# The first sublayer's start in another order: modulation in quarters, ten tiles on the operand without its norm, squares on GpSimd

## The chip, the cores and the metric

The kernel runs on one core of a Trainium2 chip. The metric is the device time of one execution in microseconds, as a median of runs. Six parts of the core matter: TensorE (PE, the matrix products), VectorE (DVE), ScalarE (ACT), GpSimd (POOL), SyncE (SP), which issues most of the loads, and the DMA engines that carry them.

## What is computed

One inference step of a network of two layers with shared weights for 128 context and 256 latent tokens of width 1024, kept on the chip as x with 384 columns. Each layer has three sublayers (feed-forward, mixer, feed-forward). What matters here is the first of all, with the modulation that scales and shifts its operand:

```python
def rmsnorm(x, g):
    r = lax.rsqrt(jnp.mean(xf * xf, axis=-1, keepdims=True) + EPS)
    return (xf * r).astype(x.dtype) * g

def swiglu(h, w13, w2):
    gate, up = jnp.split(h @ w13, 2, axis=-1)
    return (jax.nn.silu(gate) * up) @ w2

mod = jax.nn.silu(cond) @ w_mod[l] + b_mod[l]
sh1, sc1, gt1, ... = jnp.split(mod, N_MOD, axis=-1)
h = rmsnorm(x, g_norm[l, 0]) * (1.0 + sc1) + sh1
x = x + 0.5 * gt1 * swiglu(h, ffn1_w13[l], ffn1_w2[l])
```

`cond` differs between context and latent tokens, so each modulation vector has two columns. The feed-forward width is 2816.

## The kernel before, in words

Every product is made in float32 precision from halves: a number is split into a rounded high part and the low remainder. The high half of a weight is a copy on ACT (line 180), the low half a subtraction on DVE (line 183), 128x1024 each, and a product is three passes on PE (`mm3`, lines 232 to 234): high weight by high operand, low weight by high operand, high weight by low operand. **A step** is these three passes for one weight tile (128 of the 1024 rows of the output) and one of the eight parts (128 channels) of the operand. **A tile** is eight steps that add up in one PSUM buffer; its evacuation on ACT and DVE comes behind them. A feed-forward layer has 22 pairs of tiles (gate and up) in its first half. Weights come as one 512 KB load per tile through a ring of buffers; `split_upto` issues the high half at once and leaves the low half to be issued some steps later, or at once by `run_later(99)`. Jobs are generators that `step` runs one after the other, and each engine executes its instructions in the order in which the program writes them.

**The first group** (`start_group`, 287 to 370) has four tiles. `w_mod` of the scale and shift (8.4 MB) comes in four quarters; a quarter gives two of the eight parts. `products(q)` makes the sixteen small products of a quarter on PE (line 301, 256 columns, four rows of `scond` by tile position, so that four go side by side), ACT copies the result (309), `finish(q)` transposes it (316) and DVE sums it and makes `amod` (scale) and `modT` (shift). `make_h0` then scales and normalises the operand on DVE (555), adds the shift and rounds it on ACT (560), and takes the remainder on DVE (563). The norm itself is made first: squares of x on DVE and ACT at the program's start (`norm_sq`, 1190 to 1198), column sums on PE (526), the inverse root, and its broadcast to all partitions by PE (545, 546), copied as `rb` (548). So the four tiles work on the finished operand h. `warm(28)` and `warm(10)` are products without use (640) that keep PE busy.

The loads stand on SP's queue in the order x (four loads), first quarter (two loads of 1 MB), the four tiles' weights, quarters two, three and four; `cond` comes on ACT's queue.

**Later sublayers** of this kind start with `lead`: three tiles (`lead_group`) on the operand u, which is x scaled by `amod` without its norm, and 386 columns wide: the two last columns are the shift, so that their products give the shift's share apart. The norm is made meanwhile on PE (`norm_stats`, `norm_bcast`), and is applied to the result (`normed`, DVE, line 619) before the evacuation goes on with Silu on ACT (717). Five more tiles on u follow, and beside their steps `make_h` builds the normalised operand h with its scaling on POOL (575, 577) and its split on ACT and DVE (408, 411). From tile 9 on the tiles use h.

Behind the first tiles DVE makes the modulation of the other sublayers in the background (439), in pieces that `mods.put` hands out per tile: in the first sublayer over the tiles from number 8 on (counted from 0).

## Time and profile before

| | |
|---|---|
| median of 3 runs | 1919.38 us (1918.47 to 1919.88) |
| profiled execution | 1918.23 us, its span 1916.2 us |
| granted clock of PE, mean | 0.997 |
| busy share PE, its weight loads (PEld) | 99%, 97% |
| busy share DVE, ACT, POOL | 68%, 41%, 10% |

Times in the trace count from the start of the span. In the rows below, L301 is line 301 of the kernel before; "out<-in" are the program's names without buffer numbers, where S stands for buffers that share one pool (operands, and weights of the modulation's first quarters); "[0.24 <-DVE wlo L183]" says that the engine stood idle for 0.24 us just before and that the last thing it waited for was DVE's low half of a weight. Matmul records overlap one another: what a product costs in a row of equal ones is the distance of their starts, not the duration shown. The granted clock is a share of full speed: 1.00 is 2.4 GHz, 0.5 is 1.2 GHz.

### The profile page before, as it was taken

How to read it: one execution, taken by the hardware profiler on the slowest of the kernel's cores; microseconds unless marked ns; L12 is line 12 of the kernel's file. 1: busy time of each engine (PE TensorE's matmuls, PEld its weight loads, DVE VectorE, ACT ScalarE, POOL GpSimd, SP SyncE). 2: the span in 40 equal slices, each digit the busy share in tenths (PEclk: the TensorE clock that was granted, in tenths of full speed). 3: DMA queues.
4: the chain of work that ended last, by engine and by line, in shares of the span. 5: the costliest groups of instructions: out<-in, count | busy, mean ns of one | idle time of the engine just before them, and what ended most of it. 6: DMA issues, size and time to landing. Idle time of an engine off the chain costs nothing.

```text
span 1916.2 us, 28408 instructions
## 1 busy us (share of the span) xinstructions
PE 1903.4 (99%) x11024; PEld 1849.4 (97%) x11024; DVE 1308.7 (68%) x1948; ACT 789.7 (41%) x1412; POOL 198.5 (10%) x399
## 2 busy tenths in 40 slices
PE   8999999999999999999999999999999999999998
PEld 7999999889999999999999999998899999999998
DVE  5677885777656768778768779668766546655543
ACT  4433334445553444333334333354555534433332
POOL 0000003101221031000040000050022200400000
PEclk9999999999999999999999999999999999999999
DMA  8666663643335536566536656546433333354430
GB/s 331 197 200 194 219 207 128 214 131 112 98 100 173 162 112 201 189 197 223 181 109 221 192 192 223 170 137 200 123 111 103 102 123 130 111 172 157 154 110 34
DMA packets 91719, 308.69 MB, mean 161 GB/s; under 512 B 10816, under 2 KB 17600, under 8 KB 90816
## 3 DMA queue, kind: packets, MB, share of 16 engines
q1 hardware_dynamic: 90864, 306.17, 49.0%
q8 instruction: 87, 1.43, 0.3%
q10 hardware_dynamic: 720, 0.70, 0.1%
q14 instruction: 48, 0.39, 0.1%
HBM read 303.16 MB, written 3.67 MB: 160 GB/s over the span
## 4 chain that ended last, share of the span: by engine, by line
PE 98%; DMA 1%; DVE 0%; ACT 0%; issue 0%; DVEq 0%; ACTq 0%
PE mm L232 29%; PE mm L233 28%; PE mm L234 28%; PE mm L388 2%; PE mm L390 2%; PE mm L389 2%; PE sc L1009 2%; PE mm L1067 1%; PE tp L1050 1%; DMA S<-in_w_mod 1%; PE tp L835 1%; DMA gnorm<-in_g_norm 0%; PE ms L1096 0%; PE sc L301 0%; PE tp L640 0%; DMA cond<-in_cond 0%
## 5 line engine op out<-in xcount | busy, mean ns | idle before, releaser
L232 PE MATMUL mm<-S,whi 128*128 128x384 f32 (+1 forms) x3136 | 1063.8, 339 | 1.2 <-ACT S L560 1.2
L233 PE MATMUL mm<-S,wlo 128*128 128x384 f32 (+1 forms) x3136 | 1054.2, 336 | 0.2 <-DVE wlo L183 0.2
L234 PE MATMUL mm<-S,whi 128*128 128x384 f32 (+1 forms) x3136 | 1048.7, 334 | 0.0
L183 DVE TENSOR_TENSOR wlo<-raw,whi 128x1024 fp32r<-128x1024 f32 x424 | 520.6, 1229 | 239.9 <-ACT whi L180 239.2
L232 PEld LDWEIGHTS mm<-S,whi 128*128 128x128 f32 x3136 | 589.5, 188 | 14.0 <-issue 10.0
L234 PEld LDWEIGHTS mm<-S,whi 128*128 128x128 f32 x3136 | 588.8, 188 | 0.4 <-DVE S L563 0.4
L233 PEld LDWEIGHTS mm<-S,wlo 128*128 128x128 f32 x3136 | 587.6, 187 | 0.8 <-DVE wlo L183 0.6
L180 ACT ACTIVATE whi<-raw 128x1024 fp32r<-128x1024 f32 x424 | 445.5, 1052 | 199.6 <-PE mm L234 116.5
L439 DVE SCALAR_TENSOR_TENSOR acc<-raw,scond,acc 128x1024 f32<-128x1024 f32 x224 | 277.3, 1280 | 0.0
L408 ACT ACTIVATE S<-t 128x384 fp32r<-128x384 f32 x144 | 74.1, 523 | 329.7 <-DVE t L732 241.3
L509 POOL TENSOR_TENSOR yr<-yv,nhalf 128x3 f32<-128x3 f32 x9 | 9.6, 1062 | 1344.0 <-DVE yv L529 1016.6
L411 DVE TENSOR_TENSOR S<-t,S 128x384 fp32r<-128x384 f32 x144 | 83.8, 590 | 34.6 <-ACT S L408 34.6
L732 DVE TENSOR_TENSOR t<-t,mm 128x384 f32<-128x384 f32 x76 | 42.1, 554 | 77.8 <-PE mm L234 77.8
L713 ACT ACTIVATE t<-mm 128x384 f32<-128x384 f32 x76 | 37.3, 491 | 137.5 <-PE mm L234 137.5
L388 PE MATMUL mm<-whi,S 128*128 128x512 f32 x192 | 77.3, 403 | 0.0
L390 PE MATMUL mm<-whi,S 128*128 128x512 f32 x192 | 75.2, 392 | 0.0
L389 PE MATMUL mm<-wlo,S 128*128 128x512 f32 x192 | 75.1, 391 | 0.0
L577 POOL TENSOR_SCALAR t<-t,amod,modT 128x256 f32<-128x256 f32 x80 | 67.3, 850 | 4.2
L502 ACT ACTIVATE t<-x 128x384 f32<-128x384 f32 x44 | 22.9, 526 | 98.3 <-DVE x L627 98.3
L1100 DVE SCALAR_TENSOR_TENSOR S<-ms,sublng,S 128x128 fp32r<-128x128 f32 (+1 forms) x32 | 13.4, 418 | 65.3 <-ACT S L1099 65.3
L1026 ACT ACTIVATE e<-sc,ym 128x384 f32<-128x384 f32 (+1 forms) x96 | 47.7, 508 | 20.0 <-DVE ym L1016 20.0
L627 DVE SCALAR_TENSOR_TENSOR x<-mm,modT,x 128x256 f32<-128x256 f32 x96 | 35.6, 413 | 28.3 <-PE mm L234 28.0
(150 smaller groups left out, 1144.0 us busy)
## 6 DMA issues: line engine op xcount, KB each, us to landing
raw<-in_ffn_w SPq DMA_DIRECT2D x264, 512.0 KB, 4.2
raw<-in_w_mod SPq DMA_DIRECT2D x132, 512.0 KB, 4.6
raw<-in_w_in SPq DMA_DIRECT2D x112, 512.0 KB, 3.8
raw<-in_w_branch_a SPq DMA_DIRECT2D x16, 512.0 KB, 3.7
raw<-in_w_branch_b SPq DMA_DIRECT2D x16, 512.0 KB, 3.7
raw<-in_w_out SPq DMA_DIRECT2D x16, 512.0 KB, 3.7
S<-in_w_mod SPq DMA_DIRECT2D x6, 1024.0 KB, 10.7
x<-in_x SPq DMA_DIRECT2D x4, 384.0 KB, 4.2
```

Of the source, the lines that this page charges most:

```text
L180: S.activation(out=hi, in_=raw, func=AF.Copy)
L183: V.tensor_tensor(out=lo, in0=raw, in1=hi.bitcast(F32), op=ALU.subtract)
L232: T.matmul(ps, lhsT=w_hi, rhs=r_hi, start=first, stop=False)
L233: T.matmul(ps, lhsT=w_lo, rhs=r_hi, start=False, stop=False)
L234: T.matmul(ps, lhsT=w_hi, rhs=r_lo, start=False, stop=last)
L388: T.matmul(ps, lhsT=l_hi[:, kt, ts_], rhs=hi[:, sl], start=first, stop=False)
L389: T.matmul(ps, lhsT=l_hi[:, kt, ts_], rhs=lo[:, sl], start=False, stop=False)
L390: T.matmul(ps, lhsT=l_lo[:, kt, ts_], rhs=hi[:, sl], start=False, stop=last)
L408: S.activation(out=dst_hi, in_=src, func=AF.Copy)
L411: V.tensor_tensor(out=dst_lo, in0=src, in1=dst_hi.bitcast(F32), op=ALU.subtract)
L439: V.scalar_tensor_tensor(out=acc[n], in0=raw, scalar=s, in1=acc[n], op0=ALU.mult, op1=ALU.add)
L577: G.tensor_scalar(out=t[:, s0:s1], in0=t[:, s0:s1], scalar1=amod[:, i, kt, n:n + 1], scalar2=modT[:, l, pc_sh, kt, n:n + 1], op0=ALU.mult, ...
```

## The change

In the first sublayer the order of the work is now written out as a list of words, `START`, and that of the loads as another, `LOADS`:

- **Loads.** The first quarter comes ahead of x, and the quarters, parts of x and the four tiles' weights are interleaved. Each quarter comes in four loads of 512 KB. `b_mod` and `g_norm` stand with `cond` at the head of ACT's queue.
- **Products.** A quarter's sixteen products are made in four visits of four (`p00` to `p33`), one per load. All four quarters share one PSUM buffer. `finish` multiplies with a selection matrix (`tiled`) instead of transposing, and DVE makes scale and shift straight from PSUM.
- **Operand.** The four tiles work on u (`make_u`, 386 columns), and so do six more tiles behind them, with `make_h` beside: ten tiles on the operand without its norm, where there were none. `lead` does both groups; `make_h0` is gone. The exchange of two buffers' roles (`turn`) that later sublayers do now stands behind the first four tiles too.
- **Norm.** The squares are made on POOL (`q0` to `q7`, fifteen operations of 384 columns), the sums, the inverse root and the broadcast (`n0`, `n1`, `n2`) stand among the steps of the four tiles.
- **Warming products.** Ten ahead of the first visit, then groups of two to twelve (`w10`, `w3`, `w12` ...) between the visits.
- The background modulation of this sublayer starts at tile 10 instead of 8. The table of ACT's Silu function is loaded by a small dummy call at the start.

In `START` a word `s12` is a step of tile 1 with part 2, `p21` a visit of quarter 2 for its second load, `f1` finish of quarter 1, `u3` part 3 of the operand, `c2` the split of tile 2's weight (low half included), `e0` the evacuation of tile 0 and the split of the weight four tiles on. In `LOADS` `q1` is a quarter, `x2` two parts of x, and `c4` the weights' loads up to the fourth.

```diff
+LOADS = "q0 x0 c1 c2 x2 q1 c3 c4 x4 q2 x6 c7".split()
+START = (
+    "q0 q1 q2 q3 q4 q5 q6 q7 w10 p00 w3 p01 w3 p02 w3 p03 w2 f0 u0 c0 u1 c1 w12 s00 s01 s10 p10 s11 p11 w3 p12 "
+    "w3 p13 w2 f1 u2 u3 c2 c3 w5 s02 s12 s03 s13 s20 s21 p20 s22 s23 p21 s30 s31 p22 s32 p23 s33 f2 u4 u5 w2 "
+    "s04 s14 p30 s24 s34 p31 s05 p32 n0 s15 p33 s25 f3 u6 u7 n1 s35 s06 s16 s07 s17 n2 e0 e1 s26 s27 e2 s36 s37 e3"
+).split()
...
+            start_group(keys[:n0], evacs[:n0], l, i)
+            Job([], lambda c: iter_once(turn))
...
+        def products(at):
+            q, r = divmod(at, 10)
+            key = first_keys(q)[r]
+            for g in range(4):
+                T.matmul(
+                    st0["big"][32 * g:32 * g + 32, q % 2, 0:256], lhsT=scond[:, 4 * (r // 2) + g, 2 - 2 * (r % 2):34 - 2 * (r % 2)],
+                    rhs=raw_of[key][:, g * 256:(g + 1) * 256],
+                    start=r == 0, stop=r == 3, tile_position=(0, 32 * g))
...
         def finish(q):
+            m = tmp(256)
+            S.activation(out=m, in_=st0["big"][:, q % 2, 0:256], func=AF.Copy)
+            sel = st0["big"][:, q % 2, 256:264].rearrange("p (f c) -> p f c", f=2)
             for f in range(2):
+                T.matmul(sel[:, f, :], lhsT=m[:, f * P:(f + 1) * P], rhs=tiled[:, 0:4], start=True, stop=True)
+            for f in range(2):
+                k = 2 * q + f
+                V.scalar_tensor_tensor(
+                    out=amod[:, i, k, :], in0=sel[:, f, 0:2], scalar=gnorm[:, l, i, k:k + 1], in1=modT[:, l, SC1, k, :],
+                    op0=ALU.mult, op1=ALU.add)
...
+        def square(k):
+            if k == 0:
+                nst["acc"] = sp.tile([P, NT], F32, tag="at", name="acc")
+                G.tensor_tensor(out=nst["acc"], in0=x[:, k, :], in1=x[:, k, :], op=ALU.mult)
+            else:
+                sq = sp.tile([P, NT], F32, tag="qf", name="sq", bufs=2)
+                G.tensor_tensor(out=sq, in0=x[:, k, :], in1=x[:, k, :], op=ALU.mult)
+                G.tensor_tensor(out=nst["acc"], in0=nst["acc"], in1=sq, op=ALU.add)
...
+                elif what == "e":
+                    run_later(99)
+                    evacs[arg](pss[arg][:, :NU])
+                    split_upto(c + n + arg)
...
-        n_u = 0 if first else 8
-        n_0 = 4 if first else n_u
+        n_0 = 10 if first else 8
...
-        spread = 2 * NFF - 8
+        spread = 2 * NFF - n_0
...
-        for dt in range(4):
-            norm_sq(dt)
...
-            S.activation(out=sq, in_=x[:, dt, :], func=AF.Square)
```

**On PE, in the middle of the four tiles, before**: `mm_283` to `mm_286` are the four tiles' results, `sc_354` that of the second quarter's products, S0 and S1 the operand's halves, S6 and S7 buffers that hold the quarter.

```order
L232 MATMUL mm_286<-S0_150,whi_274 128x384
L233 MATMUL mm_286<-S0_150,wlo_275 128x384
L234 MATMUL mm_286<-S1_151,whi_274 128x384
L232 MATMUL mm_283<-S0_150,whi_203 128x384
L233 MATMUL mm_283<-S0_150,wlo_204 128x384
L234 MATMUL mm_283<-S1_151,whi_203 128x384
L301 MATMUL sc_354<-S6_112,scond_71 32x256 x4
L301 MATMUL sc_354<-S7_114,scond_71 32x256 x4
L301 MATMUL sc_354<-S6_112,scond_71 32x256 x4
L301 MATMUL sc_354<-S7_114,scond_71 32x256 x4
L232 MATMUL mm_284<-S0_150,whi_233 128x384
```

In before all sixteen products of a quarter stand in one row between two steps.

**The same place after**: `mm_143` and `mm_144` are the third and fourth tile, `sc_139` the result of the third quarter's products.

```order
L242 MATMUL mm_143<-S1_131,whi_308 128x386
L310 MATMUL sc_139<-S6_117,scond_71 32x256 x4
L240 MATMUL mm_144<-S0_130,whi_314 128x386
L241 MATMUL mm_144<-S0_130,wlo_315 128x386
L242 MATMUL mm_144<-S1_131,whi_314 128x386
L240 MATMUL mm_144<-S0_130,whi_314 128x386
L241 MATMUL mm_144<-S0_130,wlo_315 128x386
L242 MATMUL mm_144<-S1_131,whi_314 128x386
L310 MATMUL sc_139<-S7_120,scond_71 32x256 x4
L240 MATMUL mm_144<-S0_130,whi_314 128x386
L241 MATMUL mm_144<-S0_130,wlo_315 128x386
L242 MATMUL mm_144<-S1_131,whi_314 128x386
```

The sixteen are now four visits, with one or two steps of a tile between them.

**On ACT, around the last steps of the four tiles, before**: `t_493` is the Silu of the first tile (a gate, which becomes its product with the second tile), `whi_495` the high half of the fifth tile's weight, S0 the operand's high half, S2 the high half of that product.

```order
L560 ACTIVATE S0_150<-t_465,modT_78 128x256
L560 ACTIVATE S0_150<-t_465,modT_78 128x128
L713 ACTIVATE t_493<-mm_283 128x384
L180 ACTIVATE whi_495<-raw_262 128x1024
L408 ACTIVATE S2_504<-t_493 128x384
L713 ACTIVATE t_518<-mm_285 128x384
L408 ACTIVATE S2_504<-t_518 128x384
L180 ACTIVATE whi_529<-raw_278 128x1024
```

There the first tile's Silu and the split of the fifth tile's weight follow the operand's last part.

**The same place after**: `rb_494` is the broadcast norm, `t_496` the first tile's normalised result, `yb_497` its share of the shift, `whi_502` the high half of the fifth tile's weight, S2 again the high half of the product.

```order
L561 ACTIVATE rb_494<-ms_491 128x384
L716 ACTIVATE t_496<-t_496,yb_497 128x256
L716 ACTIVATE t_496<-t_496,yb_497 128x128
L188 ACTIVATE whi_502<-raw_237 128x1024
L421 ACTIVATE S2_508<-t_496 128x384
L188 ACTIVATE whi_517<-raw_312 128x1024
L716 ACTIVATE t_530<-t_530,yb_531 128x256
L716 ACTIVATE t_530<-t_530,yb_531 128x128
L188 ACTIVATE whi_536<-raw_318 128x1024
```

The fifth tile's weight now stands behind the norm's copy and the first tile's two Silu pieces.

**On POOL, at the program's start, before**: `ident` is the unit matrix, `yr` the norm's root of a later sublayer.

```order
masks.py:199 ISA
masks.py:199 AFFINE_SELECT ident_64<-ident_64 128x128
L509 TENSOR_TENSOR yr_193<-yv_191,nhalf_67 128x3
L509 TENSOR_TENSOR yr_2857<-yv_2855,nhalf_67 128x3
L575 TENSOR_TENSOR t_2969<-x_80,rb_2894 128x384
```

**After**: `acc` is the sum of squares, `sq` one square.

```order
masks.py:199 ISA
masks.py:199 AFFINE_SELECT ident_64<-ident_64 128x128
L337 TENSOR_TENSOR acc_145<-x_80 128x384
L340 TENSOR_TENSOR sq_147<-x_80 128x384
L341 TENSOR_TENSOR acc_145<-acc_145,sq_147 128x384
L340 TENSOR_TENSOR sq_150<-x_80 128x384
L341 TENSOR_TENSOR acc_145<-acc_145,sq_150 128x384
```

POOL now squares x in the first group, one square and one sum per part, where it had nothing to do before.

## Rows read from the trace of the kernel before

**Rows 1.** Waits of PE, whole span: times in total, count, longest, us.
```profile
PE sc L301 <- DMA S<-in_w_mod: 2.5, 2, 1.8
...
```

**Rows 2.** Stretches: length, busy us per engine, granted clock, DMA share, GB/s.
```profile
12.00:36.00 24.00, 20.75 (x166) 15.01 (x163) 14.14 (x40) 9.12 (x17) 0.80 (x1) 0.86 1.02 411
48.55:1916.20 1867.65, 1859.85 (x10695) 1813.64 (x10694) 1282.93 (x1875) 770.11 (x1373) 196.96 (x392) 1.00 0.49 157
```

**Rows 3.** PE in time order: start, duration, what, count, idle before and releaser.
```profile
12.92 2.79 PE L301 MATMUL sc<-S,scond 128*32 128x256 f32 x24 [0.71 <-DMA S<-in_w_mod]
...
20.34 0.42 PE L232 MATMUL mm<-S,whi 128*128 128x384 f32 x1
20.60 0.34 PE L233 MATMUL mm<-S,wlo 128*128 128x384 f32 x1
...
21.53 0.44 PE L233 MATMUL mm<-S,wlo 128*128 128x384 f32 x1 [0.24 <-DVE wlo L183]
...
37.17 0.33 PE L234 MATMUL mm<-S,whi 128*128 128x384 f32 x1
37.44 1.94 PE L301 MATMUL sc<-raw,scond 128*32 128x256 f32 x32
...
39.58 0.33 PE L233 MATMUL mm<-S,wlo 128*128 128x384 f32 x1
...
48.55 0.34 PE L232 MATMUL mm<-S,whi 128*128 128x384 f32 x1
...
49.07 0.34 PE L232 MATMUL mm<-S,whi 128*128 128x384 f32 x1
```

**Rows 4.** PE in time order, other stretches: warming products, norm sums, norm broadcast.
```profile
5.38 4.07 PE L640 MATMUL tp<-ones 128*128 128x128 f32 x35
...
310.98 0.73 PE L526 MATMUL ms<-ones,acc 128*128 128x2 f32 x6
...
316.12 0.60 PE L546 MATMUL ms<-t,ones 128*128 128x256 f32 x2
```

**Rows 5.** ACT and DVE by form: count | busy us, mean ns | idle.
```profile
L180 ACT ACTIVATE whi<-raw 128x1024 fp32r<-128x1024 f32 x424 | 445.5, 1052 | 199.6 <-PE mm L234 116.5 <-issue 55.7 <-PE mm L390 20.4
...
L548 ACT ACTIVATE rb<-ms 128x384 f32<-128x384 f32 x6 | 2.9, 492 | 30.0 <-PE ms L546 30.0
...
L309 ACT ACTIVATE t<-sc 128x256 f32<-128x256 f32 x4 | 1.5, 385 | 4.6 <-PE sc L301 4.6
...
L183 DVE TENSOR_TENSOR wlo<-raw,whi 128x1024 fp32r<-128x1024 f32 x424 | 520.6, 1229 | 239.9 <-ACT whi L180 239.2
...
L619 DVE TENSOR_TENSOR t<-mm,rb 128x384 f32<-128x384 f32 x24 | 13.1, 546 | 0.0
```

**Rows 6.** ACT in time order, the operand's high part for the first step.
```profile
19.05 0.80 ACT L560 ACTIVATE S<-t,modT 128x256 fp32r<-128x256 f32 x2 [0.28 <-DVE t L555]
```

**Rows 7.** PE by form, first of the three products.
```profile
L232 PE MATMUL mm<-S,whi 128*128 128x384 f32 x2816 | 954.0, 339 | 1.2 <-ACT S L560 1.2
...
L232 PE MATMUL mm<-S,whi 128*128 128x386 f32 x320 | 109.9, 343 | 0.0
```

**Rows 8.** POOL, then DVE, in time order, where POOL normalises an operand.
```profile
319.40 1.02 POOL L575 TENSOR_TENSOR t<-x,rb 128x384 f32<-128x384 f32 x1
...
321.49 1.98 POOL L575 TENSOR_TENSOR t<-x,rb 128x384 f32<-128x384 f32 x1
...
329.60 1.69 DVE L183 TENSOR_TENSOR wlo<-raw,whi 128x1024 fp32r<-128x1024 f32 x1 [1.82 <-ACT whi L180]
```

**Rows 9.** DVE in time order, a later layer's first eight tiles.
```profile
977.40 0.55 DVE L619 TENSOR_TENSOR t<-mm,rb 128x384 f32<-128x384 f32 x1
...
1002.12 1.23 DVE L183 TENSOR_TENSOR wlo<-raw,whi 128x1024 fp32r<-128x1024 f32 x1 [0.38 <-ACT whi L180]
...
1006.70 1.23 DVE L183 TENSOR_TENSOR wlo<-raw,whi 128x1024 fp32r<-128x1024 f32 x1 [1.88 <-ACT whi L180]
...
1010.79 2.55 DVE L183 TENSOR_TENSOR wlo<-raw,whi 128x1024 fp32r<-128x1024 f32 x2 [0.39 <-ACT whi L180]
```

199 lines of the change are left out of this document (71 added, 128 removed).

## The prediction

> **What bounds the kernel now.** I read three views in this order. First who keeps TensorE (PE) waiting: over the whole span there are four such groups, the dearest 2.5 us [rows 1]. Then the stretches: from 48.55 us to the end PE is busy 1859.85 of 1867.65 us [rows 2]. So the program is a start of 48.55 us and a rest that PE paces; whatever moves the instant at which the fifth weight tile begins moves the end by as much, and any new wait of PE behind it adds. Third the start itself on PE [rows 3]: the first step (three products of one weight tile with one of eight parts of the operand) begins at 20.34 (its second product at 20.60), the last of 32 steps ends at 48.55. One step in the steady state is 0.52 us (48.55 to 49.07) [rows 3], so 32 steps are 16.7 of these 28.2 us; the rest is modulation products, transposes and waits. The change rewrites this start and the six tiles behind it. Elsewhere only the pacing of the background modulation moves (26 pieces over 34 tiles instead of 36), which rests on VectorE (DVE) and is not waited for behind 48.55; I cost it at nothing.
>
> **When the first step can start.** In before the second load of the first quarter is what a product waits for until 12.92 [rows 3]; 3.67 MB were ordered up to it (1.57 of x, 2.10 of the quarter). Now the quarter comes first: 1.57 MB less, at 411 GB/s [rows 2] 3.8 us, so it is there at 9.1. Then, one behind the other: the last visit of products 0.5, the copy on ScalarE (ACT) 0.39 [rows 5], two selection products 0.5 (four records; six small ones take 0.73 [rows 4]), 0.3 allowed for three small DVE operations, on ACT the scaled operand in two pieces 0.80 [rows 6] and the weight's high half 1.05, on DVE its low half 1.23 [rows 5]. That is 14.2 for the second product of the first step. PE's own queue comes on top: ten warming products at the lower clock, then four visits with three warming products between them, which end about 1 us later than the load. I take 15.4, bounds 14.2 and 16.0; before it was 20.60 [rows 3], so **5.2 us earlier**.
>
> **What PE does from there to the end of the four tiles.**
> - Steps: 32 x 0.52, and 96 products of 386 instead of 384 columns, 4 ns longer each [rows 7]: 17.0 (before 16.7).
> - Visits to the modulation products. From 37.17 to 39.58 PE does two weight products and one visit of sixteen [rows 3]: 2.41, less two of 0.17, is 2.06 per visit. The sixteen are eight rounds; the last of the 32 records starts 1.94-0.38 = 1.56 after the first, so a round is 0.22 and eight are 1.73. Entering and leaving thus cost 0.33. Before: three visits inside this stretch, 6.2. Now four products per visit, twelve visits: 12 x (0.43+0.33) = 9.1. Lower bound 12 x 0.43 = 5.2 if the switch hides; I take 9.1, since the row shows the same neighbours.
> - Warming products on PE's queue: two groups of three in the second quarter stand between loads that have landed (1.8 us of loads apart, but PE is by then behind them). 4.07/35 = 0.116 per record [rows 4], two records each: 1.4. Those behind a quarter's last visit lie inside the next item.
> - From a quarter's last product to the next step: 0.39 + 0.5 + 0.3 + 0.8, with handovers 2.1. Behind quarter 1 nothing covers it (2.1), behind quarter 2 one step (1.6), behind quarter 3 two (1.1): 4.8. Before, the copies and transposes of later quarters stood beside steps; what PE waited there is part of its 28.2.
> - The norm: the sums 0.7 and the broadcast 0.6 [rows 4] now stand among the steps, before they stood ahead of 20.34: 1.3.
> - Waits for low halves on DVE, which makes the operand's eight low parts and four weights' while GpSimd (POOL) squares. Without POOL the rows show one such wait, 0.24 [rows 3]. Most of the twelve stand directly ahead of their step now: nine waits are 2.2, which I take; two are 0.5, twelve, with POOL's 0.46 (below) on two of them, 3.8.
> Sum 17.0+9.1+1.4+4.8+1.3+2.2 = 35.8. I count from the second product of the first step, so less 0.2: 15.4+35.6 = 51.0 against 48.55: **+2.5**. The 5.2 won by loading the quarter first are used up by more visits (2.9), warming (1.4), the norm (1.3) and gaps.
>
> POOL's squares themselves I cost at nothing on the path. Fifteen operations of this size take 1.02 each alone and up to 1.98 beside DVE [rows 8]. The last part of x is 9.96 MB down the queue: 12.92 + (9.96-3.67)/0.411 = 28.2, and four operations behind it give 32.3, 36.1 at 1.98 each. PE asks for the sum only behind the third of quarter 3's visits, near 40. Four microseconds cover it; without the cover the norm, and with it the evacuations, would be late by the difference.
>
> What POOL does to DVE is the other side: while POOL worked at 321.49 its operation took 1.98 instead of 1.02, and a weight's low half on DVE took 1.69 at 329.60 instead of 1.23 [rows 5, 8]. The Trainium skill (SBUF — State Buffer, Who interferes with whom) says why: a DVE instruction with two SBUF inputs and a GpSimd instruction that reads SBUF share one port pair, held for a whole instruction. The rows agree. By the rule, a low part that comes just behind a square's start stands for the whole 1.0 of it, and four such meetings would add 2 us to the 2.2 above; without the rule they would stay at 2.2 or under.
>
> **The turn from the fourth to the fifth tile.** Before, the first tile's evacuation and the fifth tile's split stand at once behind the first tile's end. Now both weight halves of the fifth tile sit on ACT and DVE behind the norm's broadcast: from the last product of tile 1 on, broadcast 0.6, its copy 0.49, the tile's scaling on DVE 0.55 and 0.1 allowed for a two-column copy, two Silu pieces 0.8 like the operand's in rows 6, high half 1.05, low half 1.23 [rows 5]: 4.8. PE has the broadcast and four steps, 2.7. **+2.0**, one microsecond ahead of the first product, the rest ahead of the second.
>
> **Six tiles without slack.** The later layers run this same form (three tiles, then five) and PE waits nowhere there, but DVE falls behind: the first tile's scaling stands at 977.40, the low halves of tiles 9, 10 and 11 (counted from 0) end at 1003.35, 1007.93 and, the first of two, 1012.0 [rows 5, 9], that is 25.9, 30.5 and 34.6 later for 4.25 us of PE per tile. There three weights lie ready when the chain starts; here none. Counting from the scaling, tile 4's low half is ready at 3.7; tile 9 would ask at 24.9 (1.0 of wait), tile 10 at 30.2 (0.3), and the seventh part of the normed operand, which now stands behind tile 11's low half (34.6 and 0.5 more), is wanted at 34.0, six steps into tile 10 (1.1). That is 2.4; the loss at the turn pushes POOL's and DVE's work together, so I take **3.0**, bounds 0 and 6. The 386 columns of these six tiles add 144 x 4 ns = **0.6**.
>
> **Sum.** 2.5+2.0+3.0+0.6 = +8.1 us. The profiled execution took 1918.23 (span 1916.2), so 1926.3; the median of the runs is 1.15 above it, so 1927.5.
>
> **Rivals.**
> - Faster: the loads are the bound and PE's extra work lies inside waits for them. The last quarter is 12.06 MB down the queue: 12.92 + 8.39/0.411 = 33.3. One visit, 2.1 and eight steps with the broadcast would end the fourth tile at 41.1 instead of 48.55; with the turn, the same 0.6 and no later waits that is -4.9, **1914.5**. It decides if PE's work from 15.4 up to the last visit fits into 18 us. I count 22 steps, eleven visits, warming, two gaps and the sums: 26. For it: the start is full of transfers (411 GB/s from 12 to 36). Against it: before, PE did not wait for the last quarter's loads, which were there at 37.44. Chance 0.10.
> - No change: switching hides (visits at 0.43 us, so -3.9) and ACT and DVE keep up behind the turn as in the later layers: 2.5-3.9+2.0+0.6 = +1.2, **1920.6**. For it: PE's weight loads run ahead; against it the 0.33 above. Chance 0.17.
> - Slower still: the granted clock falls. It was 0.86 in the mean from 12 to 36 [rows 2], that is 24 x 0.14 x 2 = 6.7 us at 1.2 instead of 2.4 GHz, after PE had done only small products and waited. If such 6.7 us fall among the steps, half of them is lost: +3.4, **1931**. Against it: the warming products now stand in those gaps. Chance 0.11.
> - The squares on POOL come too late, or DVE stands at every square: inside the forecast's range (waits 3.8, start 16.0: 1929.7).
>
> **How the numbers follow.** Forecast 1927.5 with 0.62: its own bounds are 1921.5 (start 14.2, waits 0.5, none behind the turn, the rest as taken) and 1932.5 (16.0, 3.8, 6). The no-change case 0.17, faster 0.10, clock 0.11. The range 1919.5 to 1932.5 holds the forecast, most of the no-change case and the clock's; out of it is the faster case and little above. A measurement of this kernel tells about 0.2% (3.8 us) from no change: the forecast case lies beyond that but for a little, so slower 0.73, within 0.2% 0.17, faster 0.10.
>
> **What would show it.** PE's first step at 13 to 15.5 us and the fifth tile at 50 to 54 (it waits about 1 for ACT, then 1 for DVE); rows of waits of PE for low halves in the first 85 us, several microseconds together; POOL busy some 15 to 20 us in the first 40; the granted clock near 1 from 6 us on; behind tile 11 no wait. I am wrong in the first sum if the fourth tile ends before 48 us, in the turn if the fifth tile follows without a gap, and in the later sum if tiles 5 to 10 show no waits.

## The result, and the profile after

The changed kernel takes 1932.42 us (median of 4 runs, 1930.91 to 1933.61) against 1919.22 for the kernel before: 13.2 us slower, a ratio of 1.0070 (95% interval 1.0057 to 1.0082). The forecast was slower by 8.1 us, 1927.5. The measured time lies at the upper end of its range or just above it: 1932.42 as measured, and 1932.8 as 1.0070 times the 1919.38 from which the forecast counted. The profiled execution took 1932.33 us with a span of 1930.6 and a granted clock of 0.997.

Waits of PE in steps over the whole span (us in total, times, longest), first in the kernel before, then in the changed kernel:

```profile
PE mm L232 <- ACT S L560: 1.2, 2, 0.7
...
PE mm L233 <- DVE wlo L183: 0.2, 1, 0.2
```

```profile
PE mm L241 <- DVE wlo L191: 2.8, 4, 1.1
PE mm L240 <- ACT S L603: 1.5, 2, 0.8
...
PE mm L242 <- DVE S L597: 1.0, 1, 1.0
PE mm L240 <- ACT whi L188: 0.9, 1, 0.9
...
PE mm L242 <- DVE S L424: 0.7, 1, 0.7
PE mm L240 <- ACT S L421: 0.6, 1, 0.6
```

Steps waited 1.4 us for ACT and DVE before, and 7.5 us now: for low halves (line 191), the operand's parts (594 to 604), the fifth tile's high half (188), and the normalised operand (421, 424). The waits for loads went the other way, from the 2.5 us of [rows 1] to 0.7. Lines 240 to 242 are the three passes of a step. PE in time order, after:

```profile
15.91 0.44 PE L241 MATMUL mm<-S,wlo 128*128 128x386 f32 x1 [0.64 <-DVE wlo L191]
...
17.87 0.44 PE L242 MATMUL mm<-S,whi 128*128 128x386 f32 x1 [1.00 <-DVE S L597]
...
19.64 0.44 PE L241 MATMUL mm<-S,wlo 128*128 128x386 f32 x1 [1.15 <-DVE wlo L191]
...
20.19 0.64 PE L310 MATMUL sc<-S,scond 128*32 128x256 f32 x8
...
26.41 0.71 PE L639 MATMUL tp<-ones 128*128 128x128 f32 x4
...
28.91 0.44 PE L240 MATMUL mm<-S,whi 128*128 128x386 f32 x1
...
36.24 0.34 PE L242 MATMUL mm<-S,whi 128*128 128x386 f32 x1
36.51 0.64 PE L310 MATMUL sc<-S,scond 128*32 128x256 f32 x8
...
37.36 0.34 PE L241 MATMUL mm<-S,wlo 128*128 128x386 f32 x1
...
38.37 0.45 PE L240 MATMUL mm<-S,whi 128*128 128x386 f32 x1
...
40.86 0.44 PE L240 MATMUL mm<-S,whi 128*128 128x386 f32 x1 [0.76 <-ACT S L603]
...
47.89 0.44 PE L240 MATMUL mm<-S,whi 128*128 128x386 f32 x1
...
50.39 0.44 PE L240 MATMUL mm<-S,whi 128*128 128x386 f32 x1 [0.69 <-ACT S L603]
...
56.58 0.44 PE L240 MATMUL mm<-S,whi 128*128 128x386 f32 x1 [0.87 <-ACT whi L188]
57.84 0.44 PE L241 MATMUL mm<-S,wlo 128*128 128x386 f32 x1 [0.82 <-DVE wlo L191]
...
89.18 0.44 PE L240 MATMUL mm<-S,whi 128*128 128x384 f32 x1 [0.56 <-ACT S L421]
...
90.50 0.44 PE L242 MATMUL mm<-S,whi 128*128 128x384 f32 x1 [0.70 <-DVE S L424]
```

The first step's second product starts at 15.91 (20.60 before, [rows 3]); the fifth tile begins at 56.58 (48.55 before) and its second product at 57.84. The last two rows are in tile 10, six steps in; tiles that are named by a number are counted from 0, so the fifth tile is tile 4. And two stretches with their clock (length, busy us per engine, clock, DMA share, GB/s):

```profile
20.19:24.41 4.22, 4.22 (x27) 2.33 (x26) 0.00 (x0) 0.00 (x0) 0.26 (x1) 0.60 1.02 407
57.84:62.14 4.30, 4.30 (x16) 4.30 (x16) 3.64 (x8) 1.47 (x2) 2.85 (x3) 0.60 0.36 122
```

A mean clock of 0.60 over 4.2 us: in steps of one microsecond it is 0.50 from 21 to 24.4 and from 58.6 to 62, and 1.00 before and after. Both times PE had just stood still: 1.00 and 1.15 us in the first steps, 0.87 and 0.82 at the turn (from the fourth to the fifth tile).

To see where the 14.4 us of span went, I put step n of one kernel beside step n of the kernel before, for all 3136 steps of this kind (start of the second product, after minus before, us). I call this difference the lag. All runs of this study are in the table, each with the lag at five steps:

| kernel | first step | fourth tile's last | fifth tile's first | tile 11's first | last | median |
|---|---|---|---|---|---|---|
| changed | -4.7 | +7.0 | +9.1 | +13.6 | +14.5 | 1932.42 |
| e1_fill | -4.7 | +7.0 | +10.6 | +13.7 | +14.4 | 1933.92 |
| e2_act_squares | -4.7 | +3.6 | +5.6 | +10.0 | +10.7 | 1928.67 |
| e3_one_visit | -4.6 | +4.4 | +6.5 | +11.1 | +11.8 | 1930.31 |
| e4_early_norm | -4.6 | +9.8 | +11.0 | +15.2 | +15.9 | 1932.49 |
| e5_split_first | -4.7 | +7.7 | +8.4 | +14.0 | +14.8 | 1934.14 |
| e6_eight | -4.7 | +8.1 | +10.2 | +21.8 | +22.6 | 1940.27 |
| e7_less_warm | -4.6 | +6.2 | +8.3 | +12.8 | +13.7 | 1931.42 |
| e8_all | -4.7 | -0.7 | -0.1 | +5.6 | +6.3 | 1924.31 |
| e9_all_ahead | -4.8 | -0.8 | -0.8 | -0.3 | +0.4 | 1918.44 |
| e10_ahead_only | -4.7 | +7.0 | +7.7 | +8.3 | +9.0 | 1928.05 |
| e11_twelve | -4.7 | +7.2 | +9.4 | +11.6 | +13.7 | 1932.19 |
| e12_weights_first | -4.7 | +2.3 | +2.4 | +3.0 | +3.8 | 1921.59 |
| e13_no_gap_warm | -4.6 | -1.3 | -1.3 | -0.9 | -0.1 | 1917.77 |
| e14_no_warm | -4.8 | -1.8 | -1.8 | -1.3 | -0.6 | 1917.35 |

So the changed kernel wins 4.7 us up to the first step, loses 11.7 in the four tiles, 2.1 at the turn and 4.5 in the six tiles behind, and under 1 in all the rest. These are differences of two profiled executions; one alone can lie a microsecond off its median, as e9_all_ahead shows (last step +0.4, median 0.8 below).

### The profile page after: what moved, and what is told of

Read it like the earlier page. It is cut to its first block, busy times and chain, and to the rows that moved or that the text cites. A ratio compares the mean times of both kernels' runs of the same rounds, so it can differ in the third digit from the quotient of the medians.

```text
span 1930.6 us, 28513 instructions
## 1 busy us (share of the span) xinstructions
PE 1913.0 (99%) x11040; PEld 1851.3 (96%) x11040; DVE 1315.6 (68%) x1961; ACT 789.7 (41%) x1422; POOL 236.2 (12%) x438
## 4 chain that ended last, share of the span: by engine, by line
PE 97%; DVE 2%; ACT 1%; issue 1%; DMA 0%; DVEq 0%; SPq 0%; ACTq 0%
PE mm L240 28%; PE mm L241 28%; PE mm L242 27%; PE mm L401 2%; PE mm L403 2%; PE mm L402 2%; PE sc L1004 2%; PE mm L1062 1%; PE tp L1045 1%; DVE wlo L191 1%; PE tp L830 1%; PE tp L639 0%; PE sc L310 0%; ACT whi L188 0%; DMA S<-in_w_mod 0%
## 5 line engine op out<-in xcount | busy, mean ns | idle before, releaser
L424 DVE TENSOR_TENSOR S<-t,S 128x384 fp32r<-128x384 f32 x152 | 88.4, 590 | 35.7 <-ACT S L421 35.7
L572 POOL TENSOR_SCALAR t<-t,amod,modT 128x256 f32<-128x256 f32 x96 | 80.5, 847 | 5.0
L570 POOL TENSOR_TENSOR t<-x,rb 128x384 f32<-128x384 f32 x48 | 57.1, 1190 | 44.2 <-ACT rb L561 26.6
```

The costliest lines, as they stand in the source:

```text
L424: V.tensor_tensor(out=dst_lo, in0=src, in1=dst_hi.bitcast(F32), op=ALU.subtract)
L572: G.tensor_scalar(out=t[:, s0:s1], in0=t[:, s0:s1], scalar1=amod[:, i, kt, n:n + 1], scalar2=modT[:, l, pc_sh, kt, n:n + 1], op0=ALU.mult, ...
```

## The experiments

Two theories stood against each other. **A**: every wait and every fall of the clock is PE's own loss, and they add up. **B**: from the first evacuation to tile 10 a chain of ACT and DVE work sets the end; PE only meets it there, so what PE wins ahead of it is given back. Within B: **B1**, the chain is slow by the order in which it is written; **B2**, DVE and POOL have more work there than PE.

**e1_fill: PE kept busy at the turn.**

```diff
- ... s36 s37 e3
+ ... s36 s37 w16 e3
```

> Sixteen warming products (1.9 us) stand on PE's queue behind the fourth tile's last step, where PE waits 2.1 us in all for ACT and DVE before the fifth tile runs. Theory A (waits bring the clock down, and what the clock costs is added to the end): the granted clock stays at 1.00 behind 58 us instead of 0.5 for 3.4 us, which gives back 1.7 us: 1930.7. Theory B (from the norm's broadcast to tile 10 a chain of ACT and DVE work sets the end, and PE only waits for it at tile 10): the clock stays up as well, but the waits of 0.6 and 0.7 us at tile 10 grow by what the clock gave, and the time stays 1932.4 within 0.5. Theory C (the fall of the clock has nothing to do with the wait): the clock falls at 58 us as before, and the time stays.

Measured 1933.92 (ratio to before 1.0078, 1.0062 to 1.0095), with a profiled span of 1930.7, that of the changed kernel (1930.6). In e1_fill PE at the turn, the stretch behind it with its clock, and PE at tile 10:

```profile
55.57 3.73 PE L640 MATMUL tp<-ones 128*128 128x128 f32 x32
...
59.31 0.34 PE L242 MATMUL mm<-S,wlo 128*128 128x386 f32 x1
...
59.20:64.00 4.80, 4.80 (x29) 4.80 (x29) 2.93 (x4) 2.66 (x5) 4.58 (x5) 1.00 0.42 124
...
89.24 0.45 PE L241 MATMUL mm<-S,whi 128*128 128x384 f32 x1 [0.57 <-ACT S L422]
```

The clock stays at 1.00 where it was 0.5, but this run does not decide between A and B. Sixteen warming products are 32 records and took 3.5 us (55.57 to the next product at 59.06), not the 1.9 of my expectation, so they outlast the wait: the fifth tile's second product starts at 59.31 instead of 57.84. They cost 1.5 us there, nearly all of the 1.7 that the clock then gives back. Both kernels leave the fifth tile within 0.2 us of each other and reach tile 10's wait together (89.24 and 89.18).

Two other runs decide it, by chance. e3_one_visit and e7_less_warm (below) have the same two waits at the turn, but their clock does not fall behind them. In e7_less_warm the turn, the stretch behind it with its clock, and PE at the first step of tile 9:

```profile
55.74 0.44 PE L240 MATMUL mm<-S,whi 128*128 128x386 f32 x1 [0.87 <-ACT whi L188]
57.00 0.45 PE L241 MATMUL mm<-S,wlo 128*128 128x386 f32 x1 [0.82 <-DVE wlo L191]
...
57.00:62.00 5.00, 5.00 (x28) 4.85 (x29) 4.17 (x8) 1.56 (x3) 3.54 (x4) 1.00 0.32 108
...
79.98 0.45 PE L241 MATMUL mm<-S,wlo 128*128 128x386 f32 x1 [0.95 <-DVE wlo L191]
```

Both runs win 1.6 us on the changed kernel in the fifth tile and have lost them again at tile 9, most of it in this wait of 0.95 us, which the changed kernel does not have. From the fourth tile to tile 11 they lose 6.7 us each, the changed kernel 6.6. So the second fall of the clock cost nothing at the end: PE meets a chain that ends when it ends, which is B for this stretch. And waits of this size are not always followed by a fall.

**e2_act_squares: the squares taken from POOL.**

```diff
- q0 q1 q2 q3 q4 q5 q6 q7 w10 ... u1 c1 w12 ... c2 c3 w5
+ w10 ... u1 c1 q0 q1 q2 q3 w12 ... c2 c3 q4 q5 q6 q7 w5
- G.tensor_tensor(out=sq, in0=x[:, k, :], in1=x[:, k, :], op=ALU.mult)
- G.tensor_tensor(out=nst["acc"], in0=nst["acc"], in1=sq, op=ALU.add)
+ S.activation(out=sq, in_=x[:, k, :], func=AF.Square)
+ V.tensor_tensor(out=nst["acc"], in0=nst["acc"], in1=sq, op=ALU.add)
```

> The squares are made by ACT and their sum by DVE, in stretches where both were idle, and POOL has no work in the first 45 us. Theory A (the first steps wait for DVE because POOL's squares run beside it): the operand's second low part takes 0.75 us instead of 2.04, the second tile's low half 1.23 instead of 1.84, the stretch from the first step's second product to the first visit of the second quarter shrinks from 4.3 to about 2.0 us; if the fall of the clock at 21 us comes from these waits, it goes too and gives 1.7 more: minus 2.3 to minus 4.0, 1928.4 to 1930.1. Rival (DVE's own work is the bound there, POOL costs nothing): the stretch stays above 3.8 us and the time within 0.5 of 1932.4.

Measured 1928.67 (1.0049, 1.0034 to 1.0064): 3.8 us less. In the changed kernel POOL's squares (337 to 341), then DVE beside them:

```profile
14.95 1.59 POOL L340 TENSOR_TENSOR sq<-x 128x384 f32<-128x384 f32 x1 [0.85 <-DMA x<-in_x]
...
18.58 1.87 POOL L341 TENSOR_TENSOR acc<-acc,sq 128x384 f32<-128x384 f32 x1
...
15.78 2.04 DVE L597 SCALAR_TENSOR_TENSOR S<-x,amod,S 128x256 fp32r<-128x256 f32 x2
17.74 1.84 DVE L191 TENSOR_TENSOR wlo<-raw,whi 128x1024 fp32r<-128x1024 f32 x1
```

And the same two pieces of DVE work in e2_act_squares, the first visit behind them, and the first step behind the second quarter:

```profile
15.75 0.74 DVE L598 SCALAR_TENSOR_TENSOR S<-x,amod,S 128x256 fp32r<-128x256 f32 x2
16.41 1.22 DVE L192 TENSOR_TENSOR wlo<-raw,whi 128x1024 fp32r<-128x1024 f32 x1
...
18.24 0.64 PE L311 MATMUL sc<-S,scond 128*32 128x256 f32 x8
...
25.47 0.44 PE L241 MATMUL mm<-S,whi 128*128 128x386 f32 x1
```

The operand's second low part, two instructions, takes 0.74 us instead of 2.04, the low half 1.22 instead of 1.84, and the visit that stood at 20.19 stands at 18.24. That is 2.0 us of the 3.8. Another 1.5 is the clock: from this visit to the first step behind the quarter e2_act_squares takes 7.23 us (18.24 to 25.47) and the changed kernel 8.72 (20.19 to 28.91), 3.4 of them at half; in e2_act_squares the clock stays at 1.00 up to 55 us. The remaining 0.3 is spread over the steps behind. The Trainium skill (SBUF — State Buffer, Who interferes with whom) has it that a DVE instruction with two SBUF inputs and a GpSimd instruction that reads SBUF shut one another out for a whole instruction. These rows agree. This gain stays to the end (3.8 us less lag at the last step): it comes ahead of the chain, and the chain moves with it.

**e3_one_visit: sixteen products in a row.**

```diff
- s10 p10 s11 p11 w3 p12 w3 p13 ... s20 s21 p20 s22 s23 p21 s30 s31 p22 s32 p23
+ s10 s11 w3 w3 p10 p11 p12 p13 ... s20 s21 s22 s23 s30 s31 s32 p20 p21 p22 p23
- s04 s14 p30 s24 s34 p31 s05 p32 n0 s15 p33
+ s04 s14 s24 s34 s05 n0 s15 p30 p31 p32 p33
```

> The sixteen products of quarters two, three and four stand in one row again, where their last visit stood; nothing else moves but the steps between them. Theory A (each entry and exit between steps and modulation products costs 0.33 us on PE): nine visits fewer, minus 2.5 to minus 3.0: 1929.4 to 1929.9. Rival (the switch hides behind weight loads or waits for transfers): the time stays within 0.7 of 1932.4.

Measured 1930.31 (1.0058, 1.0043 to 1.0073), 2.1 less: between the rival's 0.7 and the 2.5 to 3.0 of A. By the steps it is 2.6 less at the end of the fourth tile and 2.7 at the last step, which is A for the price of a visit. One visit can be read in the changed kernel's rows above: from the third pass of one step at 36.24 to the second pass of the next at 37.36 are 1.12 us, where two passes without a visit are 0.35; so 0.77, as forecast (0.76).

**e4_early_norm and e5_split_first: the turn.** The first moves the norm's sums, root and broadcast up and the first evacuation directly behind its tile; the second also puts the weight's split ahead of the evacuation, for the four first tiles.

```diff
- p22 s32 p23 s33 f2 u4 u5 w2 s04 s14 p30 s24 s34 p31 s05 p32 n0 s15 p33 s25 f3 u6 u7 n1 s35 s06 s16 s07 s17 n2 e0 e1
+ p22 n0 s32 p23 s33 f2 u4 u5 n1 w2 s04 s14 p30 s24 s34 p31 n2 s05 p32 s15 p33 s25 f3 u6 u7 s35 s06 s16 s07 e0 s17 e1
```

```diff
+                    split_upto(c + n + arg)
+                    run_later(99)
                     evacs[arg](pss[arg][:, :NU])
-                    split_upto(c + n + arg)
```

> Sums, root and broadcast of the norm stand as early as POOL's squares allow (the sums behind quarter three's third visit, near 37 us, the broadcast behind quarter four's second visit), and the first tile is evacuated directly behind its last step. Theory A (the waits at the turn, the clock and tile 10 are PE's and add up): the fifth tile follows with under 0.5 us of wait, the clock stays at 1.00 there, tile 10 waits no more: 2.1 + 1.7 + 1.9 = 5.7 us less, 1926.7. Theory B (the chain of ACT and DVE work from the first evacuation on to tile 10 sets the end): the end moves only by what the chain's start moves, from 54.2 to some 51.5 us, 2.7 us less, 1929.7, and tile 10 still waits. Rival (the norm is not ready so early, PE waits for POOL's sum): a wait ahead of the sums, and less than 2 us won.

> As e4_early_norm, and behind each of the four first tiles the split of the weight four tiles on stands ahead of the evacuation on ACT and DVE instead of behind it. Measured from the last step of the fourth tile to the first of tile 11, where the changed kernel lost 6.6 us against the kernel before and e4_early_norm 5.4. Theory B1 (the written order is what makes the chain late: a weight's halves stand behind an evacuation that waits for PE and for the other engine): the fifth tile waits under 0.4 us, the chain starts some 2 us earlier, and the loss in this stretch falls to 1.5 to 3.0 us; the time falls by 3.6 to 5.1 against the changed kernel where the first steps run as there (1927.3 to 1928.8). Theory B2 (DVE and POOL simply have more work in these six tiles than PE): the waits at tile 10 grow by what is won at the turn, and the loss stays at 4.5 or more.

Measured 1932.49 (1.0070, 1.0055 to 1.0085) and 1934.14 (1.0077, 1.0062 to 1.0092): neither won anything. In e4_early_norm a part of this is the clock in the first steps, which this edit does not touch:

```profile
18.80:25.80 7.00, 6.05 (x32) 3.24 (x35) 0.89 (x1) 0.00 (x0) 3.42 (x3) 0.52 1.03 410
```

0.52 over 7.0 us, some 6.8 us at half, where the changed kernel had 3.4. But the table also answers without it. From the last of the four tiles to tile 11 the changed kernel loses 6.6 us, e4_early_norm 5.4, e5_split_first 6.3; the turn alone costs 2.1, 1.2 and 0.7. What the turn gave was taken back behind it, as B says. For e5_split_first my expectation under B1 (1.5 to 3.0) missed, and by the numbers written there B2 had won.

**What DVE does in that stretch.** The number that B2 rests on is DVE's load. From the first tile's end to the end of tile 10's wait, in the changed kernel (the stretch; then DVE's low halves: count, busy, mean ns, idle ahead of them and what ended it):

```profile
52.40:90.50 38.10, 35.06 (x183) 33.19 (x182) 25.00 (x44) 16.69 (x29) 21.50 (x24) 0.96 0.31 99
...
L191 DVE TENSOR_TENSOR wlo<-raw,whi 128x1024 fp32r<-128x1024 f32 x8 | 11.2, 1400 | 9.0 <-ACT whi L188 8.9
```

DVE is busy for 25.00 of 38.10 us; 9.0 us of the rest it stands ahead of low halves, waiting for ACT's high halves. That is no overload. The order on ACT shown in the section on the change tells why: a high half stands behind the Silu of an evacuation, that waits for DVE's scaling, the scaling stands behind the low half before, and that waits for its high half. This makes a loop over two engines, with some 10 us for two tiles (the scaling of tile 3 at 65.73 us, of tile 5 at 75.74, of tile 7 at 85.88), where PE wants them every 8.5 (sixteen steps). Each turn of the loop loses 1.5 us. In e5_split_first I had cut it for four tiles and left it in the six behind.

**e10_ahead_only: the loop cut, and nothing else.** In all ten tiles the high half of the weight four tiles on is issued ahead of the evacuation; `ahead` is set for the six tiles behind the first four.

```diff
-                    run_later(99)
+                    split_upto(c + n + arg)
                     evacs[arg](pss[arg][:, :NU])
-                    split_upto(c + n + arg)
+                    run_later(99)
...
                 yield
+            if ahead:
+                split_upto(c + W_BUFS)
             evac(ps[:, :n])
```

> The changed kernel with one edit of order alone: behind each of its ten first tiles the high half of the weight four tiles on is issued on ACT ahead of that tile's evacuation, and in the first four its low half directly behind it. No work is added or taken away; the squares, the visits and the late norm stay. Theory B1 (the written order closes a loop: a high half stands on ACT behind a Silu that waits for DVE's scaling, which stands on DVE behind the low half before): DVE, busy 25.0 of the 38.1 us between the first tile's end and tile 10, loses less of the rest to ACT's high halves (9.0 us now); the loss from the fourth tile's last step to tile 11 falls from 6.6 to between 1.5 and 3 us, and the time to 1927.4 to 1928.8. Theory B2 (POOL and DVE in each other's way set the pace of these tiles): the loss stays over 5 us and the time above 1930.8.

Measured 1928.05 (1.0045, 1.0030 to 1.0060), 4.4 less. The same stretch in e10_ahead_only, DVE's low halves in it, and the one wait of PE behind the fourth tile:

```profile
52.40:85.10 32.70, 32.16 (x183) 31.80 (x182) 26.95 (x47) 17.89 (x30) 27.68 (x24) 1.00 0.42 130
...
L192 DVE TENSOR_TENSOR wlo<-raw,whi 128x1024 fp32r<-128x1024 f32 x9 | 11.4, 1268 | 0.4 <-ACT whi L189 0.4
...
56.47 0.45 PE L242 MATMUL mm<-S,wlo 128*128 128x386 f32 x1 [0.54 <-DVE wlo L192]
```

The stretch shrinks from 38.10 to 32.70 us. DVE waits 0.4 us for high halves instead of 9.0, PE waits 0.54 at the turn, the clock does not fall there, and tile 10 has no wait. The loss from the fourth tile to tile 11 is 1.3 us, under the expected 1.5 to 3. B1 is shown, B2 is out: POOL is busier in this stretch than it was (27.68 us of 32.70) and does no harm. The norm is as late as in the changed kernel here, so its place was not the cause.

**e6_eight and e11_twelve: how many tiles on the operand without its norm.**

```diff
-        n_0 = 10 if first else 8
+        n_0 = 8                      (e6_eight)
+        n_0 = 12 if first else 8     (e11_twelve)
```

> Eight tiles on the operand without its norm instead of ten: four, and four more with the normalised operand made beside them (two of its parts per tile instead of four in three tiles). Theory B (the chain of evacuations, weight splits and operand parts is late from the turn on and PE meets it where the normalised operand is asked for): the wait moves from tile 10 to tile 8 and is as large or larger, 2 to 4 us instead of 1.9, less 0.2 for fewer wide products: 1932 to 1934.5. Rival (six tiles without slack are too many, four are bearable): no wait at tile 8, 1930.3.

> Twelve tiles on the operand without its norm instead of ten, nothing else: the eight parts of the normalised operand are spread over eight tiles instead of six. With eight tiles the time was 8 us more than with ten. Theory B1 and B2 agree that the wait for the operand shrinks or goes, from 1.9 us to under 0.7, with 0.2 us more for wide products: 1930.8 to 1931.6. Rival (the weights' halves, not the operand's parts, are what comes late in the loop): the wait is there again at tile 10 to 12, as a wait for a low half, and the time stays at 1932.4 or rises.

e6_eight: 1940.27 (1.0107, 1.0090 to 1.0124). PE at tile 8 in e6_eight:

```profile
82.71 0.59 PE L241 MATMUL mm<-S,whi 128*128 128x384 f32 x1 [2.56 <-ACT S L422]
...
84.35 0.69 PE L243 MATMUL mm<-S,whi 128*128 128x384 f32 x1 [0.73 <-DVE S L425]
```

The place was right, the size not: the time rises by 7.9 us, where I had expected waits of 2 to 4 us instead of 1.9. The operand is asked for two tiles earlier, and from tile 8's first step to tile 9's the lag grows by 8.0 us, part of it at half the clock (0.51 on average from 82.7 to 93.1 us), which the durations of 0.59 and 0.69 us show. e11_twelve: 1932.19 (1.0068, 1.0052 to 1.0084), as the changed kernel, and not the 1930.8 to 1931.6 that I had expected. The wait at tile 10 goes, and in tile 12's last step there stands

```profile
98.58 0.44 PE L243 MATMUL mm<-S,whi 128*128 128x384 f32 x1 [0.70 <-DVE S L425]
```

with 1.3 us more of lag between tile 11 and tile 16. Twelve tiles only put off the meeting with the loop. With the loop cut there is no wait at ten.

**e7_less_warm, e13_no_gap_warm, e14_no_warm: the warming products.** The first takes two groups of three out of the changed kernel, the second the same two out of e9_all_ahead (below), the third all behind the first step.

```diff
- s11 p11 w3 p12 w3 p13 w2 f1
+ s11 p11 p12 p13 w2 f1        (e14_no_warm: no w2 here, and no w5, w2 behind)
```

> Only the two groups of three warming products between the visits of the second quarter are left out. Theory A (they stand on PE's queue while the loads have long landed): the stretch from 20.2 to the end of the quarter's last visit at 26.4 us shrinks by their 1.7 to 2.6 us (one group ran at half the clock), and the time by as much, 1929.8 to 1930.7. Rival 1 (they fill waits for the loads): the time stays, and PE shows waits for the loads instead. Rival 2 (they hold the clock): the stretch at half the clock grows from 3.4 to 5 us or more, and half of what is won is lost.

> e9_all_ahead without the two groups of three warming products between the visits of the second quarter (0.87 us each on PE's queue). Theory A (pure cost: the loads have landed): 1.5 to 1.8 us less, 1916.6 to 1916.9, and the granted clock stays at 1.00. Rival 1 (they fill waits for the loads): waits for transfers of together over 1 us, and the time within 0.5 of 1918.4. Rival 2 (they hold the clock): a stretch at half the clock between 20 and 30 us, and 1918 or more.

> As e13_no_gap_warm, and the groups behind the finishes and ahead of the steps that wait for the operand (two, five, two) are left out as well; those ahead of the first step stay. Theory A (these stand beside ACT's and DVE's work and cost nothing, nor do they hold anything): the same as e13_no_gap_warm within 0.4 us. Rival (they hold the clock: without them PE stands idle for some 2 us behind the second quarter's finish, and the clock falls a few us later): a stretch of some 3.4 us at half the clock in the steps behind, 1.5 to 1.9 us more than e13_no_gap_warm.

e7_less_warm: 1931.42 (1.0061, 1.0046 to 1.0076), 1.0 less. The stretch from 18.8 us in it:

```profile
18.80:25.80 7.00, 6.08 (x38) 2.73 (x39) 0.87 (x1) 0.06 (x1) 3.31 (x3) 0.52 1.03 410
```

Again some 6.8 us at half, in place of 3.4. I could not tell from this run whether the missing products had done it, since e4_early_norm, which has them, shows the same row. So the same edit was made where the clock does not fall: e13_no_gap_warm takes 1917.77 against 1918.44 for e9_all_ahead, 0.7 less and not 1.5 to 1.8; the clock stays at 1.00, and PE's waits for transfers are now (0.5 us, once, in e9_all_ahead):

```profile
PE sc L313 <- DMA S<-in_w_mod: 1.3, 2, 0.7
```

One of the two, 0.62 us at 21.33, stands in the second quarter; the other is in the first, where e9_all_ahead has its own. So Theory A and rival 1 each held in part: of the 1.74 us on PE's queue 0.7 came off the time, and at least 0.6 had filled a wait for loads. e14_no_warm, 1917.35, is 0.4 us less, within A's 0.4 and inside the noise of the two, but not for A's reason. In e14_no_warm

```profile
25.00:28.60 3.60, 3.60 (x14) 3.60 (x13) 3.11 (x4) 2.12 (x4) 0.00 (x0) 0.53 1.03 408
```

the clock falls for 3.4 us behind a wait of 1.31 us for ACT, as the rival said. The 1.5 to 1.9 us that the rival gave for this do not show in the time. I take it that as much came back because the steps no longer queue behind warming products; no run separates the two.

**e8_all, e9_all_ahead, e12_weights_first: the remedies together.** e8_all has the squares of e2_act_squares, the third and fourth quarter in one visit each with steps behind the visit to cover its finish, the early norm, and the split order of e5_split_first; e9_all_ahead has that of e10_ahead_only instead; e12_weights_first also loads two weights ahead of the second quarter, puts eight steps there instead of four, and has more warming products: a third group of three between the visits, and ten and four behind the second and third quarter instead of five and two. The order of e8_all and e9_all_ahead, then the loads of e12_weights_first:

```diff
+ ... s02 s12 s03 s13 s20 s21 s22 s23 p20 p21 p22 p23 s30 f2 s31 s32 s33 u4 u5 n0 w2 s04 s14 s24 s34 n1
+ p30 p31 p32 p33 s05 f3 s15 s25 s35 u6 u7 n2 s06 s16 s07 e0 s17 e1 s26 s27 e2 s36 s37 e3
...
- LOADS = "q0 x0 c1 c2 x2 q1 c3 c4 x4 q2 x6 c7".split()      (e12_weights_first only)
+ LOADS = "q0 x0 c1 c2 x2 c3 c4 q1 x4 q2 x6 c7".split()
```

> All at once: squares on ACT and DVE (3.8 us in the run by itself), one visit each for the third and fourth quarter, with steps between the visit, its finish and the parts that it gives, so that PE does not wait for those (2.0 for six visits, 1.6 for two waits), early norm and split ahead of evacuation (3.6 to 5.1). Theory A with B1 (the prices add up): 1932.4 less 11.0 to 12.5, that is 1919.9 to 1921.4, and the fourth tile ends near 48 us. Rival (what is won in the first four tiles is given back in the six behind them, where DVE and POOL are the bound): no earlier than 1924.

> As e8_all (the fourth tile ended 0.7 us ahead of the kernel before, and 6.3 us were lost from there to tile 11), with the high halves ahead of the evacuations as in e10_ahead_only. B1: the loss falls to 1 to 2.5 us and the time to 1919.3 to 1920.8, level with the kernel before. B2: it stays at 1923 or more.

> As e9_all_ahead, and the third and fourth tile's weights are loaded ahead of the second quarter, so that eight steps on the first two parts lie between the first and the second quarter's products instead of four. Theory (PE has work for four steps in a stretch in which it warmed or waited, the last loads come no later): the fourth tile ends 1.5 to 2.5 us earlier than in e9_all_ahead, 1917 to 1918.5 in all, under the kernel before. Rival (the second quarter lands 2.6 us later and everything behind it with it): no gain or a loss of up to 1 us.

e8_all: 1924.31 (1.0026, 1.0016 to 1.0035). The four tiles end 0.7 us ahead of the kernel before, and 6.3 are lost behind: the rival's side, since the loop was still there. e9_all_ahead: 1918.44 (0.9996, 0.9986 to 1.0005), 14.0 us under the changed kernel and level with the kernel before. All waits of PE in it:

```profile
PE mm L242 <- DVE wlo L192: 1.3, 3, 0.6
PE tp L642 <- DVE nhalf L1167: 1.0, 1, 1.0
PE sc L313 <- DMA S<-in_w_mod: 0.5, 1, 0.5
```

From tile 0 to the end only 1.3 us of waits are left. With two groups of warming products less (e13_no_gap_warm, 0.9990, 0.9981 to 0.9999) or five (e14_no_warm, 0.9992, 0.9983 to 1.0000) it is a tenth of a per cent faster than the kernel before, at the edge of what can be told. So the repairs bring the new order level with the old one; no run here shows it clearly ahead.

e12_weights_first, 1921.59 (1.0012, 1.0002 to 1.0022), missed its expectation by 3 us or more, and the rival's as well (a loss of up to 1 us; it is 3.2 over e9_all_ahead). PE in it, the second quarter's last visit and the warming behind its finish:

```profile
26.34 0.64 PE L313 MATMUL sc<-S,scond 128*32 128x256 f32 x8
...
27.95 2.48 PE L642 MATMUL tp<-ones 128*128 128x128 f32 x20
```

In e9_all_ahead that visit stood at 22.27. It falls back by 4.1 us: four steps (2.1) that are pulled forward, a wait of 0.80 for a low half at 20.95, and the third group of warming products (0.87). The steps are saved again later, the wait and the group are not, and the longer group behind the finish adds 1.1 (2.48 against 1.36 us). That is 2.8 of the 3.1 us by which the fourth tile ends later than in e9_all_ahead. PE shows no wait for loads there; the same order with fewer warming products was not tried.

## Why the prediction was wrong, step by step

The step that failed is the sum for the four tiles: +2.5 forecast at their end, +7.0 measured. The first five points take it apart; the changed kernel's rows in the section on the result and those of e2_act_squares are their source.

- **The first step.** 15.91 for its second product, forecast 15.4 (14.2 to 16.0): held, 0.5 late. The terms listed for it add up to 13.9, not to the 14.2 given.
- **Steps, visits, the norm.** 0.53 us a step and 0.77 a visit were right, and e3_one_visit confirms that a visit's entry and exit (2.6 us for nine, 0.29 each against 0.33) is paid on PE. POOL's sum of squares came in time: the norm's sums on PE did not wait for it.
- **Waits for DVE.** The sum took 2.2 us. From 15.91 to the first visit at 20.19 PE needs 4.28 us for eight passes of 0.18, so some 2.8 are lost to waits there; with 0.2 to 0.3 at a later low half it is 3.1, or 0.9 more than the sum had. In e2_act_squares the same stretch takes 2.35 us (15.89 to 18.24). So POOL adds 2.0 us, as much as the prediction named beside its sum, in two pieces of DVE work (1.30 and 0.62 us longer) and not in four meetings. Without POOL the waits would have been half of the 2.2: the base was too high, the effect of the squares was left out, and the two errors partly cancelled.
- **The clock.** The sum had no fall of the clock; a rival had it at 0.11, worth 3.4 us, "half of 6.7". It fell twice for 3.4 us. The first fall cost 1.5 us (8.72 against 7.23 in the second quarter), the second nothing, as e3_one_visit and e7_less_warm show. The forecast counted the waits and did not ask what may follow them: nine kernels of this study have the two waits of about 1 us in the first steps, and in all nine the clock fell there; in the six whose waits there are about 0.5 us it did not.
- **Gaps behind the finishes.** The forecast had 2.1 us from a quarter's last product to the step that needs it, all three times. Measured are 2.5, all three times (26.41 to 28.91, 38.37 to 40.86, 47.89 to 50.39, with no step, one and two steps in between). That makes 5.9 us for the 4.8 taken. Two groups of warming products, 1.4 us in the sum, were worth 0.7 where they were left out (e13_no_gap_warm).

So of the 4.5 us by which the four tiles came out later, 0.5 is the start, 0.9 the waits for DVE, 1.5 the clock and 1.1 the gaps; the last 0.5 is spread.

- **The turn.** +2.0 forecast, +2.1 measured, with the two waits in the order named. It is the one step that came out to the tenth, and it was still of no use by itself: repaired alone (e5_split_first), its gain was taken back.
- **Six tiles without slack.** 3.0 taken with bounds 0 and 6, plus 0.6 for wide products; the lag grew by 4.5 from the fifth tile to tile 11: 1.8 in the fifth tile, at half the clock, and 1.9 at tile 10, where the forecast had put the last of its waits. Place and size were near, the reason was wrong. I read [rows 9] as DVE falling behind under its work; DVE was idle for a third of the time (25.00 of 38.10 us), and the loop in the written order held it. Had I put the busy share beside the lag, the repair would have been in view ahead of the experiments.
- **The background modulation** was costed at nothing. From tile 11 to the end the changed kernel loses another 0.9 us, and so do the other versions (0.7 to 0.9, e11_twelve 2.1, part of it its wait at tile 12). What in that stretch costs it was not tried.
- **The no-change rival** asked that switching hides and that ACT and DVE keep up; neither held. **The faster rival** asked that PE's work fit between loads; in e13_no_gap_warm, with the loop cut and no squares on POOL, the fourth tile ends 1.3 us ahead of the kernel before, not 7.
- **The range.** Its upper end is a little low by its own terms: 1927.5 with 0.6, 1.6 and 3.0 on top is 1932.7, not 1932.5.

The forecast had the sign and the places. It fell short by 5 us, most of it in the four tiles: the clock's fall stood in a rival and POOL's effect on DVE beside the sum, and each gap was 0.4 us too short. That it came as near as it did is partly luck, since the 2.2 for DVE and the 3.0 for the six tiles each stood for something else than what was there.

## What to carry to other kernels

When an engine falls behind in a stretch, look at its busy share there before calling it overloaded: DVE at two thirds with 9 us of waits for ACT was a loop in the written order, and issuing the weight's high half ahead of the evacuation gave 4.4 us without adding work. A gain ahead of such a chain's end is only worth what the chain moves, so find that end (here tile 10) and ask of every repair whether it reaches it. Work that is free on an idle engine can be dear for its neighbour: fifteen operations for the squares on POOL cost 3.8 us, through DVE and the clock. And work out how long a filler is from its rows before reading a result from it: the one in e1_fill cost as much as it gave.

## What the runs showed of the hardware

In the first steps the granted clock went to half (1.2 GHz) in all nine kernels whose PE stood still twice for about 1 us (0.99 to 1.01, then 0.85 to 1.15): for 3.4 us in the changed kernel, e1_fill, e3_one_visit, e5_split_first, e10_ahead_only and e11_twelve, and for some 6.8 us in e4_early_norm, e6_eight and e7_less_warm. In the six kernels with waits of about 0.56 and 0.47 us it stayed at 1.00 there; in one of these, e14_no_warm, it fell for 3.4 us behind a later wait of 1.31. At the turn, waits of about 0.87 and 0.82 us were followed by a fall of 3.4 us in the changed kernel, e2_act_squares, e6_eight and e11_twelve and by none in e3_one_visit and e7_less_warm; what decides this is not shown. In e6_eight, behind waits of 2.56, 0.73 and 1.61 us, the clock was at half for some 10 us, and in the kernel before, at its start, for some 6.7. And the two DVE instructions of an operand's low part took 2.04 us beside POOL's squares and 0.74 without them, more than the third by which a larger instruction was longer in [rows 8] (1.69 against 1.23 us).
